# Hybrid decoder layer on one core: the step-size product with upper and lower weight parts side by side

## The chip, the cores and the metric

The kernel runs on one core of a Trainium2 chip. A core has TensorE (PE in the profile), VectorE (DVE), ScalarE (ACT), GpSimd (POOL) and SyncE (SP, which here only issues transfers). Each engine works through its own list of instructions in order; semaphores hold an instruction until what it needs is done. The metric is the time of one execution in device microseconds (us). Numbers are float32 at the inputs and outputs.

## The reference

The reference is one layer of a hybrid decoder: 16 meta tokens stand ahead of 1024 tokens of width 1024, and three groups of heads work side by side on the same normalised input.

```python
hn = rmsnorm(h, mix_norm_g[i])
proj = hn @ w_in[i].astype(dt)
sb_q, sb_k, sb_v, ssm_z, ssm_xbc, ssm_dt, c_q, c_kv, k_r = jnp.split(proj, split_at, axis=-1)
o_sb = stick_breaking_attention(...)          # 8 heads of 64
o_ssm = ssd_mixer(ssm_z, ssm_xbc, ssm_dt, ...) # state space, 16 heads of 64
...
k_rope = apply_rope(k_r, cos[None], sin[None])
o_mla = mla_attention(q_mla, k_mla, v_mla, valid)  # 8 heads, latent keys
h = h + jnp.concatenate([o_sb, o_ssm, o_mla], axis=-1) @ w_out[i].astype(dt)
fn = rmsnorm(h, ffn_norm_g[i])
h = h + (jax.nn.silu(fn @ w_gate[i]) * (fn @ w_up[i])) @ w_down[i]
return rmsnorm(h, final_norm_g)[:, BLOCK:, :]
```

Two small outputs of the large projection matter here: `ssm_dt`, 16 columns, from which `ssd_mixer` makes the step sizes (`dt = softplus(dt_raw + dt_bias)`), and `k_r`, 32 columns, the rotary part of the latent attention's keys. `apply_rope` splits the 32 into two halves x1 and x2 and returns x1 cos - x2 sin and x1 sin + x2 cos, so each output half needs both input halves.

## The kernel before

All activations are held feature by feature: 128 features on the partitions, tokens along the free axis. To keep float32 accuracy on PE, every operand is split into an upper part in a shorter float format (`hi`, the rounded value) and a lower part (`lo`, the remainder), and a product is three matmuls: upper times upper, lower weight times upper input, upper weight times lower input. The normalised input is held as eight upper tiles `HH` and eight lower tiles `HL`. `dense_fm` (L136) does a product: for each chunk of tokens, eight steps along the 1024 features with three matmuls each (L144, L145, L146) into one bank of PSUM (`d_ps`, two banks in turn), and then an evacuation that the caller gives. `load_w` (L126) brings a weight block by DMA, ACT makes the upper part (L131), POOL the lower one (L133).

The tokens (1040 with the meta tokens) go in three chunks, `CH_ALL`: 272, 384 and 384.

`step_sizes` (L419) computes the step sizes and the rotary keys together. Its weight block has 96 columns: 16 for the steps, 16 of zeros, 32 for the keys, and the same 32 again with their two halves swapped. Per chunk 24 matmuls make a result of 96 rows. In the evacuation ACT adds the bias to the 16 step rows (`dtx`, L425), copies all 96 rows (`krt`, L427) and sends rows 32 to 96 to the scratch `s_kr` in HBM (L428); PE then transposes the steps block by block into the PSUM tile `dtt` (L431). Behind the last chunk a polynomial of some 20 small instructions on DVE with two on ACT makes the softplus (L435 to L458).

Much later, before the latent attention's projections, SP loads `s_kr` (64 rows) and a table of cosines and sines (L894, L895), DVE multiplies rows 0 to 32 and the swapped rows 32 to 64 with the table and adds them (L896 to L898), and the turned keys go to `s_krot` (L899).

Around this product stands the first part of the stick-breaking attention: `sb_row` makes scores on PE (`sc_ps`, L692, L693), a sigmoid on ACT (L694) and a running product on DVE (L696); `weighted_values` multiplies the weights with the values. Between, `dense_fm` makes K and Q of the next pair of heads; `k_evac` (L600) casts and subtracts each K chunk twice, on ACT (L604, L605) and DVE (L606, L607). The order on every engine is set by a scheduler that simulates the program when it is built and takes the readiest instruction by priority; `tc.high_priority` moves an evacuation forward. So an edit in one place can change the order in others.

The later stages are: the convolutions and the other pairs (to some 440 us), the state-space stage with the latent projections as filling work (to some 640 us), the latent attention, the output product and the feed-forward part.

## Time and profile before

| what | value |
|---|---|
| median of three runs | 1745.81 us (1743.37 to 1752.36) |
| profiled execution | 1744.0 us, its span 1742.3 us, mean granted PE clock 0.989 |
| PE busy | 1688.7 us, 97% of the span |
| DVE, ACT, POOL busy | 1140.2, 846.0, 717.3 us |
| DMA | 222.35 MB, mean 128 GB/s |
| PE idle 480 to 640 us | 6.5 us |

The span is the time between the first and the last instruction that the profiler recorded. A row of a group gives the line, the engine, the operation with output and inputs, the shape and the count, the busy time, and the idle time ahead of it with what ended it. Rows in order of time begin with start and length in us; matmul lengths overlap, so the distance of two starts is what one costs. A form such as 128*96 is the part of PE's array in use, rows by columns. DVE's idle time costs nothing by itself; it matters where PE waits for DVE.

### The profile page before, as it was taken

The numbers are of one execution on the slowest core, as the hardware profiler recorded it, in microseconds if no ns is written. First come the engines' busy times: TensorE is split into PE (matmuls) and PEld (weight loads), VectorE is DVE, ScalarE is ACT, GpSimd is POOL, SyncE is SP. The second block draws the span as 40 slices with busy tenths as digits, with TensorE's granted clock in tenths as the row PEclk, the third lists the DMA queues.
The fourth block names the chain that finished last, engine by engine and source line by source line (L and its number), as shares of the span: only waits on it lengthen the run. The fifth ranks groups of instructions, "written<-read, shape, count | busy, mean of one in ns | idle before, by whom it ended". The sixth has DMA issues, their size and how long they took to land.

```text
span 1742.3 us, 26429 instructions
## 1 busy us (share of the span) xinstructions
PE 1688.7 (97%) x9673; PEld 1479.6 (85%) x9673; DVE 1140.2 (65%) x1773; ACT 846.0 (49%) x1811; POOL 717.3 (41%) x514
## 2 busy tenths in 40 slices
PE   8889999999999999999999999999999999999998
PEld 7879989999987888998888878788888888878887
DVE  7777676678455644556576556966666656688644
ACT  6555565656477727776455425432223222343333
POOL 3233335344567537553331445635555555200012
PEclk9999999999999999999999999999999999999999
DMA  4321232122534465348222452232322233999602
GB/s 164 72 67 62 69 89 80 59 69 78 154 115 121 149 219 167 107 130 282 68 78 65 103 180 73 70 99 92 114 91 97 96 104 106 328 398 358 235 1 98
DMA packets 145639, 222.35 MB, mean 128 GB/s; under 512 B 24722, under 2 KB 84148, under 8 KB 145508
## 3 DMA queue, kind: packets, MB, share of 16 engines
q1 hardware_dynamic: 126112, 205.09, 36.6%
q10 hardware_dynamic: 19396, 15.56, 2.9%
q8 instruction: 76, 1.25, 0.3%
q14 instruction: 55, 0.45, 0.1%
HBM read 157.56 MB, written 63.04 MB: 127 GB/s over the span
## 4 chain that ended last, share of the span: by engine, by line
PE 80%; DVE 6%; DMA 6%; ACT 3%; issue 2%; POOL 2%; SPq 0%; ACTq 0%; DVEq 0%; POOLq 0%
PE d_ps L144 9%; PE d_ps L146 9%; PE d_ps L145 9%; PE b_ps L1283 8%; PE b_ps L1282 8%; PE b_ps L1281 8%; PE b_ps L1566 2%; PE b_ps L1567 2%; PE b_ps L1565 2%; PE ptg L326 2%; PE ptg L328 1%; PE pv L305 1%; PE pv L304 1%; DMA raw<-s_osbl 1%; PE sc_ps L991 1%
## 5 line engine op out<-in xcount | busy, mean ns | idle before, releaser
L144 PE MATMUL d_ps<-hnh,whi 128*128 128x384 f32 (+6 forms) x744 | 247.4, 333 | 7.8 <-DVE KS L607 5.4
L146 PE MATMUL d_ps<-hnl,whi 128*128 128x384 f32 (+6 forms) x744 | 248.4, 334 | 0.0
L145 PE MATMUL d_ps<-hnh,wlo 128*128 128x384 f32 (+6 forms) x744 | 246.7, 332 | 0.1
L133 POOL TENSOR_TENSOR wlo<-wraw,whi 128x1024 fp32r<-128x1024 f32 (+1 forms) x57 | 136.8, 2401 | 218.2 <-ACT whi L131 194.1
L144 PEld LDWEIGHTS d_ps<-hnh,whi 128*128 128x128 f32 (+1 forms) x744 | 141.0, 190 | 12.7 <-issue 6.0
L146 PEld LDWEIGHTS d_ps<-hnl,whi 128*128 128x128 f32 (+1 forms) x744 | 140.8, 189 | 3.1 <-issue 0.7
L145 PEld LDWEIGHTS d_ps<-hnh,wlo 128*128 128x128 f32 (+1 forms) x744 | 140.9, 189 | 2.8 <-POOL wlo L133 0.4
L1282 PE MATMUL b_ps<-T,wl 128*128 128x512 f32 x352 | 139.6, 397 | 1.3 <-POOL wl L1113 1.3
L1283 PE MATMUL b_ps<-T,wh 128*128 128x512 f32 x352 | 139.2, 397 | 1.3 <-DVE T L1113 1.3
L1281 PE MATMUL b_ps<-T,wh 128*128 128x512 f32 x352 | 139.3, 397 | 0.0
L312 DVE TENSOR_TENSOR pl<-ptg,ph 128x512 fp32r<-128x512 f32 (+1 forms) x160 | 99.8, 628 | 55.3 <-ACT ph L311 54.1
L1112 ACT CAST op<-raw 128x1024 fp32r<-128x1024 f32 x69 | 71.2, 1050 | 111.3 <-PE d_ps L1567 55.1
L311 ACT CAST ph<-ptg 128x512 fp32r<-128x512 f32 (+1 forms) x160 | 85.6, 542 | 52.3 <-PE ptg L328 32.8
L1113 DVE TENSOR_TENSOR op<-raw,op 128x1024 fp32r<-128x1024 f32 x69 | 84.9, 1240 | 39.5 <-ACT op L1112 39.4
L696 DVE TENSOR_TENSOR_SCAN cm<-cm,sb_mask 128x144 f32<-128x144 f32 (+3 forms) x64 | 97.1, 1523 | 7.4 <-ACT cm L694 6.8
L1113 POOL TENSOR_TENSOR wlo<-raw,whi 128x1024 fp32r<-128x1024 f32 x18 | 45.4, 2521 | 110.3 <-ACT whi L1112 110.3
L1113 POOL TENSOR_TENSOR wl<-raw,wh 128x512 fp32r<-128x512 f32 x46 | 74.9, 1635 | 30.5 <-ACT wh L1112 30.3
L1112 ACT CAST wh<-raw 128x512 fp32r<-128x512 f32 x88 | 53.2, 616 | 69.5 <-PE b_ps L1283 69.4
L131 ACT CAST whi<-wraw 128x1024 fp32r<-128x1024 f32 (+1 forms) x57 | 58.9, 1033 | 55.4 <-PE d_ps L146 30.6
L1119 POOL TENSOR_TENSOR tt<-tt 128x512 f32<-128x512 f32 (+1 forms) x8 | 8.1, 1015 | 188.4 <-ACT tt L1637 188.2
L1282 PEld LDWEIGHTS b_ps<-T,wl 128*128 128x128 f32 x352 | 66.8, 190 | 17.4 <-POOL wl L1113 1.6
L1116 DVE TENSOR_TENSOR raw<-raw 128x512 f32<-128x512 f32 x58 | 53.2, 925 | 43.3 <-DMA raw<-in_w_gate_dram 38.4
(440 smaller groups left out, 5120.0 us busy)
## 6 DMA issues: line engine op xcount, KB each, us to landing
raw<-in_w_down_dram SPq DMA_DIRECT2D x99, 256.0 KB, 5.3
s_hops<-gs SPq DMA_DIRECT2D x63, 256.0 KB, 2.0
raw<-s_hops SPq DMA_DIRECT2D x63, 256.0 KB, 5.4
raw<-in_w_gate_dram SPq DMA_DIRECT2D x22, 512.0 KB, 3.6
raw<-in_w_up_dram SPq DMA_DIRECT2D x22, 512.0 KB, 4.2
wraw<-in_w_o_dram SPq DMA_DIRECT2D x16, 512.0 KB, 3.8
wraw<-in_w_xbc_dram SPq DMA_DIRECT2D x12, 512.0 KB, 4.2
s_xs<-csig SPq DMA_DIRECT2D x24, 192.0 KB, 2.6
```

Source lines behind the costliest of these rows:

```text
L133: pool.tensor_tensor(lo[:, :cols], raw[:, :cols], f32(hi[:, :cols]), op=ALU.subtract)
L144: pe.matmul(ps[:m, :n], wh, mh, start=(kt == 0), stop=False)
L145: pe.matmul(ps[:m, :n], wl, mh, start=False, stop=False)
L146: pe.matmul(ps[:m, :n], wh, ml, start=False, stop=(kt == nkt - 1))
L311: act.copy(ph[:, :n], pt[:, :n])
L312: dve.tensor_tensor(pl[:, :n], pt[:, :n], f32(ph[:, :n]), op=ALU.subtract)
L696: dve.tensor_tensor_scan(rev, rev, sb_mask[:, T - n_all :][:, ::-1], 1.0, ALU.mult, ALU.max)
L1112: act.copy(hi, value)
L1113: eng.tensor_tensor(lo, value, f32(hi), op=ALU.subtract)
L1281: pe.matmul(banks[j], hi[:, ks], UH[u][k], start=start and k == 0, stop=False, skip_group_check=skip)
L1282: pe.matmul(banks[j], lo[:, ks], UH[u][k], start=False, stop=False, skip_group_check=skip)
L1283: pe.matmul(banks[j], hi[:, ks], UL[u][k], start=False, stop=stop and k == 3, skip_group_check=skip)
```

## The change

The weight block of the step-size product has 64 columns now: 16 for the steps, 16 of zeros and 32 for the keys, without the swapped copy. Its upper and lower parts lie side by side, 64 and 64 columns, in one tile. One matmul with all 128 columns against the upper input makes the upper-weight product in rows 0 to 64 of the bank and the lower-weight product in rows 64 to 128; a second matmul with the 64 upper columns against the lower input adds to rows 0 to 64. That is two matmuls a step, not three. The evacuation copies rows 64 to 128 to SBUF on ACT, adds them to rows 0 to 64 on DVE, adds the bias to the 16 step rows on ACT and sends 32 rows to `s_kr`. The load of the keys is three transfers now, which put the two halves a second time, swapped, under the first.

```diff
-    s_kr = dram.tile([64, T], F32, name="s_kr")
+    s_kr = dram.tile([32, T], F32, name="s_kr")
...
-        def dt_evac(ps, c0, n):
-            dtx = fill_tile("cacc", "dtx")
-            act.activation(dtx[:16, :n], ps[0:16, :n], AF.Identity, bias=dtb)
-            krt = fill_tile("csig", "krt")
-            act.copy(krt[:96, :n], ps[:96, :n])
-            act.dma_start(s_kr[:, c0 : c0 + n], krt[32:96, :n])
...
-        dense_fm(dpool, load_w(a["w_dt"], KT * 96), KT, 96, hn_mov, CH_ALL, dt_evac)
+        raw = wa.tile([128, 1024], F32, tag="wraw", bufs=1, name="wraw")[:, : KT * 64].rearrange("p (k m) -> p k m", k=KT)
+        both = wa.tile([128, 1024], F32R, tag="whi", name="wdt").rearrange("p (k e m) -> p k e m", k=KT, e=2)
+        sp.dma_start(raw, a["w_dt"].rearrange("p (k m) -> p k m", k=KT))
+        act.copy(both[:, :, 0], raw)
+        pool.tensor_tensor(both[:, :, 1], raw, f32(both[:, :, 0]), op=ALU.subtract)
+        for c0, n in CH_ALL:
+            ps = bank()
+            for kt in range(KT):
+                mh, ml = hn_mov(kt, c0, n)
+                whole = both[:, kt].rearrange("p e m -> p (e m)")
+                if kt > 0:
+                    pe.matmul(ps[:64, :n], both[:, kt, 0], ml, start=False, stop=False)
+                pe.matmul(ps[:, :n], whole, mh, start=(kt == 0), stop=(kt == KT - 1))
+                if kt == 0:
+                    pe.matmul(ps[:64, :n], both[:, kt, 0], ml, start=False, stop=False)
+            with tc.high_priority(offset=1000):
+                low = fill_tile("cacc", "low")[:64]
+                act.copy(low[:, :n], ps[64:128, :n])
+                krt = fill_tile("csig", "krt")[:64]
+                dve.tensor_tensor(krt[:, :n], ps[:64, :n], low[:, :n], op=ALU.add)
+                dtx = fill_tile("cacc", "dtx")
+                act.activation(dtx[:16, :n], krt[0:16, :n], AF.Identity, bias=dtb)
+                act.dma_start(s_kr[:, c0 : c0 + n], krt[32:64, :n])
...
-        sp.dma_start(kx[0:64], s_kr)
+        for r0, r1, h0 in ((0, 32, 0), (32, 48, 16), (48, 64, 0)):
+            sp.dma_start(kx[r0:r1], s_kr[h0 : h0 + r1 - r0])
...
-    wdt96 = np.concatenate([wdt, zero, wkr, wkr[:, 16:], wkr[:, :16]], axis=1)
+    wdt64 = np.concatenate([wdt, zero, wkr], axis=1)
```

The scheduler places the instructions anew. On PE, in the first chunk of the product, this stood before (`hnh` and `hnl` are the upper and lower input, `whi` and `wlo` the parts of the weights):

```order
L144 MATMUL d_ps<-hnh_129,whi 96x272
L145 MATMUL d_ps<-hnh_129,wlo 96x272
L146 MATMUL d_ps<-hnl_137,whi 96x272
L144 MATMUL d_ps<-hnh_130,whi 96x272
L145 MATMUL d_ps<-hnh_130,wlo 96x272
L146 MATMUL d_ps<-hnl_138,whi 96x272
```

and this stands there now (`wdt` is the tile with both parts):

```order
L434 MATMUL d_ps<-hnl_138,wdt 64x272
L435 MATMUL d_ps<-hnh_130,wdt 128x272
L434 MATMUL d_ps<-hnl_139,wdt 64x272
L435 MATMUL d_ps<-hnh_131,wdt 128x272
L434 MATMUL d_ps<-hnl_140,wdt 64x272
L435 MATMUL d_ps<-hnh_132,wdt 128x272
```

Two matmuls a step took the place of three, and widths of 64 and 128 take turns. On ACT, where the first K chunk of the next pair is cast and the polynomial's exponential needs its table, the order before was (`d` is the polynomial's argument, `cm` a row of sigmoids, `ph` the upper part of the weights):

```order
L604 CAST K<-d_ps 64x272
L605 CAST KS<-d_ps 64x272
L443 ACT_TABLE_LOAD
L443 ACTIVATE d_1005<-d_1005 128x144
L360 CAST V<-vst 16x2x64 x2
L604 CAST K<-d_ps 64x272
L605 CAST KS<-d_ps 64x272
L694 ACT_TABLE_LOAD
L694 ACTIVATE cm<-sc_ps 128x256
L694 ACTIVATE cm<-sc_ps 128x400
L311 CAST ph<-ptg 128x384
```

and now (lines behind the edit are 15 higher: L619 is the K cast, L709 the sigmoid, L458 the exponential):

```order
L360 CAST V<-vst 128x8x64
L619 CAST K<-d_ps 64x272
L620 CAST KS<-d_ps 64x272
L619 CAST K<-d_ps 64x272
L620 CAST KS<-d_ps 64x272
L709 ACTIVATE cm<-sc_ps 128x256
L709 ACTIVATE cm<-sc_ps 128x400
L311 CAST ph<-ptg 128x384
L709 ACTIVATE cm<-sc_ps 128x384
L457 ACTIVATE d_986<-dx 128x144
L458 ACT_TABLE_LOAD
L458 ACTIVATE d_986<-d_986 128x144
```

Three sigmoids and a cast moved ahead of the exponential's table load, and a cast of values stands ahead of the K casts. On DVE, from the division by 2 + d on, the order before was:

```order
L447 RECIPROCAL d_1006<-d_1006 128x144
L606 TENSOR_TENSOR K<-d_ps,K 64x272
L607 TENSOR_TENSOR KS<-d_ps,K 64x272
L448 TENSOR_TENSOR d_1005<-d_1005,d_1006 128x144
L696 SCALAR_TENSOR_TENSOR cm<-cm,sb_mask 128x656
L312 TENSOR_TENSOR pl<-ptg,ph 128x384
L449 TENSOR_TENSOR d_1006<-d_1005 128x144
L450 TENSOR_SCALAR DT<-d_1006 128x144
L606 TENSOR_TENSOR K<-d_ps,K 64x384
L607 TENSOR_TENSOR KS<-d_ps,K 64x384
L452 SCALAR_TENSOR_TENSOR DT<-DT,d_1006 128x144
L696 SCALAR_TENSOR_TENSOR cm<-cm,sb_mask 128x784
```

and now:

```order
L462 RECIPROCAL d_987<-d_987 128x144
L621 TENSOR_TENSOR K<-d_ps,K 64x384
L622 TENSOR_TENSOR KS<-d_ps,K 64x384
L711 SCALAR_TENSOR_TENSOR cm<-cm,sb_mask 128x784
L463 TENSOR_TENSOR d_986<-d_986,d_987 128x144
L621 TENSOR_TENSOR K<-d_ps,K 64x384
L622 TENSOR_TENSOR KS<-d_ps,K 64x384
L464 TENSOR_TENSOR d_987<-d_986 128x144
```

The polynomial's steps moved behind the second K chunk's subtractions. The state-space stage, at 440 to 560 us, is placed anew too; its instructions are the same.

## The prediction

> **What bounds the kernel now.** I read the page first (engine totals and the chain of waits), then the busy time in stretches, then what PE waited for.

> ```profile
> PE 1688.7 (97%) x9673; PEld 1479.6 (85%) x9673; DVE 1140.2 (65%) x1773; ACT 846.0 (49%) x1811; POOL 717.3 (41%) x514
> PE 80%; DVE 6%; DMA 6%; ACT 3%; issue 2%; POOL 2%; SPq 0%; ACTq 0%; DVEq 0%; POOLq 0%
> 73.00:88.00 15.00, 15.00 (x87) 13.73 (x86) 3.18 (x4) 3.65 (x11) 5.18 (x6) 0.85 0.43 84
> 91.50:115.50 24.00, 19.74 (x95) 16.96 (x96) 21.17 (x35) 14.86 (x30) 11.11 (x10) 0.93 0.25 67
> 132.00:460.00 328.00, 325.14 (x2258) 314.81 (x2258) 234.84 (x339) 194.78 (x447) 130.67 (x100) 1.00 0.25 72
> 480.00:640.00 160.00, 153.51 (x1117) 127.66 (x1116) 92.57 (x159) 105.39 (x301) 96.02 (x68) 1.00 0.46 146
> 600.00:640.00 40.00, 36.37 (x209) 30.69 (x209) 21.31 (x32) 13.01 (x23) 13.37 (x7) 1.00 0.61 218
> ```

> In a row of stretches the columns after the length are PE, PEld, DVE, ACT and POOL, then the granted clock. PE is busy 97% of the span and is 80% of the chain, so a matmul saved is time saved unless a wait takes its place. The stage of the change, 73 to 88 us, is pure PE: 15.00 of 15.00 us, with DVE and ACT nearly idle. Right behind it the picture turns: from 91.5 to 115.5 us DVE is busy 21.17 of 24 us and PE has holes. From 132 to 460 us PE is full again (325.14 of 328), so what is won ahead of 132 us is carried to 460 us. The state-space stage (480 to 640 us) leaves PE 6.5 us idle, which bounds what a new order there could win; 3.6 of it lie in the last 40 us.

> **What the product costs.** The product's matmuls, by the trace in order of time (start, length, instruction):

> ```profile
> 72.44 0.58 PE L692 MATMUL sc_ps<-K,Q 128*128 128x256 f32 x1 [6.03 <-ACT cm L694]
> 73.49 0.43 PE L144 MATMUL d_ps<-hnh,whi 128*96 128x272 f32 x1
> 73.71 0.43 PE L145 MATMUL d_ps<-hnh,wlo 128*96 128x272 f32 x1
> ...
> 77.51 0.28 PE L144 MATMUL d_ps<-hnh,whi 128*96 128x272 f32 x1
> 77.63 0.29 PE L145 MATMUL d_ps<-hnh,wlo 128*96 128x272 f32 x1
> ...
> 78.26 0.34 PE L144 MATMUL d_ps<-hnh,whi 128*96 128x384 f32 x1
> 78.43 0.34 PE L145 MATMUL d_ps<-hnh,wlo 128*96 128x384 f32 x1
> ```

> Lengths overlap in the pipeline, so the price is the distance of starts: 0.175 us for 384 columns, 0.125 for 272, and 0.227 for 272 right after the 6.03 us of idle (the granted clock of 73 to 88 us is 0.85: the first 4.9 us after the idle run at half speed, until about 77.3). The new matmuls are 128 or 64 weight columns wide instead of 96. For that:

> ```profile
> 145.44 0.28 PE L305 MATMUL pv<-pl,V 128*64 128x256 f32 x1
> 145.56 0.28 PE L304 MATMUL pv<-ph,V 128*128 128x256 f32 x1
> 145.68 0.28 PE L305 MATMUL pv<-pl,V 128*64 128x256 f32 x1
> ```

> Matmuls 64 and 128 weight columns wide take turns here and start every 0.12 us for 256 streamed columns, next to 0.125 for 272 with 96: the price follows the streamed columns, not the width. So 24 of 72 matmuls go at full price. First chunk: 24 matmuls took 73.49 to 78.26 = 4.77 us; 16 at half speed take 3.63 and end at 77.1, still inside the slow spell, which saves 1.1. Second and third chunk: 8 fewer each, 16 x 0.175 = 2.8. **Term 1: -3.9 us.** Bounds: -3.8 (all at full speed) and -4.6 (all of the first chunk's eight at half speed); the alternation as a cost is a rival below.

> **The evacuation.** Per chunk ACT did a biased copy and a 96-row copy; now ACT copies the lower half, DVE adds it, ACT adds the bias. The nearest rows of the shapes:

> ```profile
> 83.06 0.57 ACT L425 ACTIVATE dtx<-d_ps,dtb 16x384 f32<-16x384 f32 x1 [1.56 <-PE d_ps L146]
> 83.54 0.45 ACT L427 COPY krt<-d_ps 96x384 f32<-96x384 f32 x1
> 99.47 0.47 ACT L604 CAST K<-d_ps 64x384 fp32r<-64x384 f32 x1
> 101.40 0.55 DVE L606 TENSOR_TENSOR K<-d_ps,K 64x384 fp32r<-64x384 f32 x1
> ```

> Before: 0.57 + 0.45; after: 0.47 + 0.55 until the bank is free, 0.57 more until the transposes may start. The bank comes free as early as before; the transposes' operand comes about 1.0 us later, under the next chunk's sixteen matmuls (2.8 us), and DVE, which takes the add, is busy only 3.18 of the stage's 15 us. Nothing on the path: 0, and about 1 us per chunk (3 us) if that cover were gone. The weights' cast and subtraction shrink by a third, ahead of use: 0.

> **The load of the keys.** Two more issues stand on SP's queue, ahead of the table's load:

> ```profile
> 458.86 0.47 SPq L894 DMA_DIRECT2D kx<-s_kr  x1
> 459.38 0.59 SPq L895 DMA_DIRECT2D ktab<-in_k_tab_dram  x1
> 466.91 1.23 DVE L898 TENSOR_TENSOR kx<-kx,ky 32x1040 f32<-32x1040 f32 x1
> 469.31 1.23 DVE L751 CAST sel<-seli 80x2048 bf16<-80x2048 f32 x1 [1.17 <-DMA xs<-s_xs]
> ```

> An issue takes 0.52 us, so the table and DVE's three products come 1.04 us later and end at 469.2 instead of 468.14. The next DVE instruction waits until 469.31 for another transfer anyway. 0, or up to +1.0 if that slack of 1.17 shrinks.

> **The list behind the product.** PE's two waits for DVE before 116 us, and what ACT, DVE and POOL did:

> ```profile
> 106.96 0.47 PE L144 MATMUL d_ps<-hnh,whi 128*128 128x512 f32 x1 [2.69 <-DVE KS L607]
> 115.50 0.47 PE L144 MATMUL d_ps<-hnh,whi 128*128 128x512 f32 x1 [0.74 <-DVE KS L607]
> 87.97 0.62 ACT L360 CAST V<-vst 128x512 fp32r<-128x512 f32 x1 [3.98 <-POOL vst L414]
> 93.14 1.28 ACT L443 ACT_TABLE_LOAD   x1
> 93.16 0.43 DVE L606 TENSOR_TENSOR K<-d_ps,K 64x272 fp32r<-64x272 f32 x1 [1.26 <-ACT KS L605]
> 94.79 0.92 DVE L446 TENSOR_SCALAR d<-d 128x144 f32<-128x144 f32 x1 [0.76 <-ACT d L443]
> 104.36 1.30 DVE L452 SCALAR_TENSOR_TENSOR DT<-DT,d 128x144 f32<-128x144 f32 x1
> 111.28 2.23 DVE L454 TENSOR_SCALAR DT<-DT 128x144 f32<-128x144 f32 x1
> 113.54 0.31 DVE L455 SCALAR_TENSOR_TENSOR DT<-dx,DT 128x144 f32<-128x144 f32 x1
> 114.80 0.56 DVE L607 TENSOR_TENSOR KS<-d_ps,K 64x384 fp32r<-64x384 f32 x1
> 111.02 2.40 POOL L133 TENSOR_TENSOR wlo<-wraw,whi 128x1024 fp32r<-128x1024 f32 x1 [1.32 <-ACT whi L131]
> ```

> PE's start at 115.50 is set by DVE's list, which runs from 93.16 to 115.36: K's subtractions mixed with the step sizes' polynomial. The list begins when PE's first K chunk is out, so term 1 moves it; but on ACT a cast of values stands between, which waited for POOL until 87.97 and whose feeding transfers do not move: it ends at 88.6, and two K casts of at most 0.47 us behind it end at 89.5, where term 1 alone would have them end at 89.24 (the table load begins behind them at 93.14, less 3.9): +0.3. Within the list nothing is added (its three additions fall ahead of it). DVE's idle 0.76 us waited for the exponential behind a table load; now sigmoids, a scan and a subtraction stand ahead of that step and fill it: -0.8. Two steps are stretched, 1.30 and 2.23 us where a neighbour takes 0.31, 2.9 us in all; the long one ends with POOL's subtraction (113.42). Each step now meets POOL at another moment; I take half, -1.4, between 0 and -2.9, or +2.9 if as many more are hit. **Term 2: +0.3 - 0.8 - 1.4 = -1.9 us**, from -3.4 (PE's waits of 2.69 and 0.74 gone) to +3.9 (PE's whole gain waited away).

> **State-space stage.** The scheduler also reorders 440 to 560 us: early groups stand behind two to three us more of dense matmuls, and from the twelfth group on the places agree again. Work and tail are the same: 0, between -3 and +10.6 (below).

> The sum: -3.9 - 1.9 = -5.8 us against the profiled execution's 1744.0 us (span 1742.3 and 1.7 around it): 1738.2. The median of the runs, 1745.81, lies 1.8 above it, so on the runs' scale I predict **1740 us**.

> **Rivals.**
> 1. *A wait takes the place.* DVE's list keeps its length or grows by hits from POOL, and PE, earlier at the second Q chunk, waits there instead. 21.17 busy of 24 us speak for it; against it, the list's head moves with PE's K chunk. With +2.9 in place of -1.4 the sum is -1.5: about 1744 (1743 to 1746).
> 2. *Switching width drains PE.* The widths change 14 times per chunk, 42 times in all. The transposes, of another shape, show what a change can cost:

> ```profile
> 82.11 0.33 PE L145 MATMUL d_ps<-hnh,wlo 128*96 128x384 f32 x1
> 82.37 0.30 PE L431 MATMUL dtt<-identr,dtx 16*16 16x16 f32 x3
> ```

> 0.26 us instead of 0.175, so 0.085 a change; 42 of them are 3.6 us and leave -5.8 + 3.6 = -2.2: 1744. The even 0.12 us at 145 us speaks against it. [...]
> 3. *The holes close.* Both waits go (term 2 at -3.4), the half-speed spell behind them too (granted clock 0.93 of 24 us: 1.7), and the state-space stage gives 3 of its 6.5: -12.0, 1734. For it: DVE alone causes them; against it: DVE stays nearly as full.
> 4. *Slower: the state-space groups run short of cover.* Dense matmuls used early are missing between the fifth and twelfth group, where a group's own chain (POOL, ACT, DVE) is then bare on PE. If two such groups each leave 3.6 us idle, as the stage's end does now, and a half-speed spell of 1.7 as above behind it, that is +10.6; it decides from +5.8 on. -5.8 + 10.6 = +4.8: 1751. For it: PE already idles 6.5 us there; against it: the places agree again from the twelfth group on.

> **How the numbers follow.** Forecast 0.56 (its own range 1735 to 1744), rival 1 0.20, rival 2 0.03, rival 3 0.12, rival 4 0.09. About 0.5%, 8.7 us, is what a measurement of this kernel can tell from no change. Faster by more: rival 3 and the forecast's tail, 0.17; slower by more: rival 4 with a third such group, 0.05; within: 0.78. The range from 1731 to 1749 holds the forecast, rivals 1 and 2, most of rival 3 and a part of rival 4.

> **What would show it.** Right: 48 matmuls with starts 0.175 us apart in the second and third chunk; DVE's list under 22 us long and the second Q chunk starting 5 to 6 us before 115.50; PE's idle in the state-space stage near 6.5 us. Wrong: starts 0.26 us apart at width changes; waits on DVE's K subtractions that grow by what PE saved; holes of over 2 us between the fifth and twelfth group.

## The result, and the profile after

The changed kernel takes 1755.57 us (median of 9 runs, 1753.65 to 1757.82), the kernel before beside it 1747.06 (9 runs, 1743.37 to 1752.36). The ratio is 1.0052 [1.0037, 1.0067]: slower by half a per cent, where 1740 us was forecast and 1749 was the upper end. The profiled execution took 1754.85 us with a span of 1753.1, which is 10.85 more than the profiled execution before (1744.0); the medians differ by 8.5.

The page's engine totals and its chain of waits, after:

```profile
PE 1690.6 (96%) x9649; PEld 1478.2 (84%) x9649; DVE 1141.9 (65%) x1776; ACT 845.7 (48%) x1811; POOL 721.8 (41%) x514
PE 70%; DVE 11%; DMA 6%; ACT 5%; issue 4%; POOL 3%; SPq 1%; ACTq 0%; DVEq 0%; POOLq 0%
```

There are 24 matmuls fewer, as the change says, and yet PE is busy 1.9 us longer; DVE's share of the chain goes from 6% to 11%. The busy time in stretches, after (columns as above):

```profile
73.00:88.00 15.00, 15.00 (x89) 13.68 (x87) 4.02 (x7) 5.94 (x14) 5.33 (x7) 0.83 0.42 83
91.50:115.50 24.00, 19.10 (x82) 15.97 (x82) 19.78 (x32) 13.23 (x26) 11.20 (x9) 0.86 0.28 82
132.00:460.00 328.00, 323.67 (x2235) 312.80 (x2234) 233.08 (x334) 193.16 (x445) 129.37 (x100) 0.99 0.25 72
480.00:640.00 160.00, 150.35 (x1096) 123.05 (x1094) 89.61 (x150) 105.78 (x302) 98.54 (x69) 1.00 0.45 142
1060.00:1160.00 100.00, 95.38 (x419) 76.47 (x420) 83.15 (x104) 41.61 (x69) 53.77 (x33) 0.95 0.23 72
```

The last of these stretches before:

```profile
1060.00:1160.00 100.00, 97.40 (x418) 78.58 (x417) 88.91 (x110) 42.49 (x73) 55.98 (x33) 0.95 0.21 65
```

The stage of the product is as full as before. Behind it the granted clock is 0.86 where it was 0.93; PE loses 1.5 us of busy time between 132 and 460 us, 3.2 in the state-space stage and 2.0 at 1060 to 1160.

Stretches of equal times hold different work once a kernel is shifted. So I matched the instructions of PE of two traces by what they do and their turn, and took how much later each starts than in the kernel before (both set to zero at 40 to 60 us; medians of each stretch). A falling number is a gain, a rising one a loss:

| us later than before at | 83–88 | 100–106 | 140–200 | 250–440 | 632–640 | 700–780 | 1030–1045 | 1180–1380 | 1640–1700 |
|---|---|---|---|---|---|---|---|---|---|
| after | -3.9 | -5.8 | -3.1 | 0.5 | 5.7 | 6.6 | 6.5 | 9.9 | 10.2 |

The change wins 5.8 us up to 106 us, and then loses 2.7 at 106 to 126 us, 3.6 at 215 to 241, 5.2 in the state-space stage, 0.9 behind it, 3.4 at the start of the feed-forward stage, and 0.2 between. The sum is +10.2 of the 10.85. Each loss is looked at in turn.

**The gain.** The product's matmuls in the second and third chunk, after (start, length, instruction):

```profile
78.31 0.34 PE L434 MATMUL d_ps<-hnl,wdt 128*64 128x384 f32 x1
78.48 0.34 PE L435 MATMUL d_ps<-hnh,wdt 128*128 128x384 f32 x1
78.66 0.34 PE L434 MATMUL d_ps<-hnl,wdt 128*64 128x384 f32 x1
```

They start 0.17 and 0.18 us apart with 64 and 128 weight columns in turn, as with 96 before.

**The loss at 106 to 126 us.** The second Q chunk, at 115.50 before, starts at 110.80. Directly ahead of it stands the matmul of the running sums (`acum`), first before and then after:

```profile
114.25 0.51 PE L464 MATMUL acum<-d,tri 128*128 128x144 f32 x2
...
109.54 0.85 PE L479 MATMUL acum<-d,tri 128*128 128x144 f32 x2 [3.15 <-DVE d L473]
110.80 0.76 PE L144 MATMUL d_ps<-hnh,whi 128*128 128x512 f32 x1 [0.41 <-DVE KS L622]
```

That wait of PE and three successive stretches of 3.41 us, after (the first number behind the length is PE's busy time, the granted clock is the third from the end):

```profile
PE acum L479 <- DVE d L473: 3.2, 1, 3.2
105.33:108.74 3.41, 1.06 (x5) 0.54 (x3) 3.33 (x5) 1.53 (x3) 3.03 (x2) 1.00 0.25 29
108.74:112.16 3.42, 2.21 (x5) 1.66 (x6) 2.78 (x7) 0.42 (x1) 0.00 (x0) 0.50 0.33 129
112.16:115.57 3.41, 3.41 (x9) 2.63 (x8) 0.69 (x1) 0.16 (x1) 0.00 (x0) 0.50 0.00 0
```

The running sums need the steps that DVE's list computes; PE, which has fewer matmuls ahead of them and does the first Q chunk at full speed now, is 8 us ahead there and waits 3.2 us. It is busy for only 1.06 of 3.41 us, and then two stretches run at half speed, over most of the second Q chunk. In the kernel before there is one such stretch here, of 3.41 us from 108.13, over the first Q chunk.

**The loss at 215 to 241 us.** 1.0 us of it goes in small pieces at 215 to 225, 1.0 in one wait at 234 us and 1.5 in a half-speed spell behind that wait. A weight load of 512 KB and the cast that waits for it, and what PE then waits for, first before and then after:

```profile
224.62 0.36 SPq L129 DMA_DIRECT2D wraw<-in_w_sbq_dram  x1
228.41 1.05 ACT L131 CAST whi<-wraw 128x1024 fp32r<-128x1024 f32 x1 [2.82 <-DMA wraw<-in_w_sbq_dram]
...
PE d_ps L144 <- DVE KS L607: 1.9, 1, 1.9
```

```profile
223.16 0.36 SPq L129 DMA_DIRECT2D wraw<-in_w_sbq_dram  x1
227.90 1.05 ACT L131 CAST whi<-wraw 128x1024 fp32r<-128x1024 f32 x1 [4.16 <-DMA wraw<-in_w_sbq_dram]
...
PE d_ps L144 <- DVE KS L622: 2.9, 1, 2.9
```

The load is issued 1.46 us earlier, but from issue to cast it takes 4.74 us, not 3.79, and PE's wait behind it grows from 1.9 to 2.9 us. The DMA queues in those 4.7 us, after, show one transfer more that does not belong to the kernel's data (count, MB, share of 16 engines):

```profile
q8 instruction: 1, 0.02, 2.0%
```

The profile names that queue `instruction`: 76 transfers of 16 KB (1.25 MB) in the whole program, for 2 x 9649 instructions of PE alone, so one in about 254 instructions of PE; with PE's semaphore instructions counted in, 256 start between two transfers on average, before and after. After, one runs from 1.03 us behind the load's issue for 1.51 us; before, it began 2.56 us ahead of the issue and was over. The longer wait leaves PE busy for 1.01 us of the 3.41 from 235.04, and the next stretch, from 238.45, runs at half speed; before, PE was busy for 1.56 us of the 3.41 from 234.42, and the granted clock stayed 1.00. The pieces at 215 to 225 are lost in the kernels whose weight load holds a code transfer (0.8 to 1.2 us) and in the others not (0.2 at most); why was not tried.

**The loss in the state-space stage.** Of PE's waits from 440 to 645 us, these lines grew; before, and after:

```profile
PE yd L841 <- DVE L L821: 1.2, 3, 0.7
...
PE R L794 <- ACT L L806: 1.0, 2, 0.7
```

```profile
PE yd L856 <- DVE L L836: 2.6, 2, 1.3
PE R L809 <- ACT L L821: 2.5, 6, 0.5
PE d_ps L144 <- ACT lrow L750: 1.5, 1, 1.5
...
PE yd L856 <- DVE dec L812: 1.0, 2, 0.6
...
PE yd L856 <- DVE ea L841: 0.5, 1, 0.5
```

2.2 us became 8.1; the other lines give 1.1 of it back. No wait is long, the granted clock is 1.00: many groups each wait 0.5 to 1.5 us for their own chain.

**The loss at the start of the feed-forward stage.** DVE in order of time, before and after (`hT` is the residual input, `raw` the scaled one, `sq` a sum of squares):

```profile
1059.03 2.72 DVE L1153 SCALAR_TENSOR_TENSOR hT<-hT,gffn,d_ps 128x512 f32<-128x512 f32 x4 [0.20 <-PE d_ps L173]
1061.67 1.53 DVE L1119 TENSOR_TENSOR sq<-sq 128x512 f32<-128x512 f32 x1
1063.12 1.78 DVE L1113 TENSOR_TENSOR raw<-hT,raw 128x512 fp32r<-128x512 f32 x1
```

```profile
1067.70 2.47 DVE L1135 TENSOR_TENSOR sq<-sq 128x512 f32<-128x512 f32 x1 [1.80 <-ACT sq L1411]
1070.10 2.71 DVE L1169 SCALAR_TENSOR_TENSOR hT<-hT,gffn,d_ps 128x512 f32<-128x512 f32 x4
1072.73 1.33 DVE L1129 TENSOR_TENSOR raw<-hT,raw 128x512 fp32r<-128x512 f32 x1
```

The addition of the squares stands ahead of the four scalings now; it waits 1.80 us for ACT, and four instructions that were ready wait with it. PE then waits 1.17 us for `raw` and 0.50 for a square, and the half-speed spell behind this place lasts 6.83 us, where it lasted 3.41 before: some 2 us are lost ahead of the spell and 1.5 more in it.

### The profile page after: what moved, and what is told of

It reads as the page before. It is cut to its first block, busy times and chain, and to the rows that moved or that the text cites. A ratio compares the mean times of both kernels' runs of the same rounds, so it can differ in the third digit from the quotient of the medians.

```text
span 1753.1 us, 26377 instructions
## 1 busy us (share of the span) xinstructions
PE 1690.6 (96%) x9649; PEld 1478.2 (84%) x9649; DVE 1141.9 (65%) x1776; ACT 845.7 (48%) x1811; POOL 721.8 (41%) x514
## 3 DMA queue, kind: packets, MB, share of 16 engines
q8 instruction: 76, 1.25, 0.3%
## 4 chain that ended last, share of the span: by engine, by line
PE 70%; DVE 11%; DMA 6%; ACT 5%; issue 4%; POOL 3%; SPq 1%; ACTq 0%; DVEq 0%; POOLq 0%
PE d_ps L144 8%; PE d_ps L146 8%; PE d_ps L145 8%; PE b_ps L1297 6%; PE b_ps L1298 6%; PE b_ps L1299 6%; PE b_ps L1582 2%; PE b_ps L1583 2%; PE b_ps L1581 2%; PE ptg L326 2%; PE ptg L328 1%; PE pv L305 1%; PE pv L304 1%; ACT L L821 1%; DMA raw<-s_hops 1%
## 5 line engine op out<-in xcount | busy, mean ns | idle before, releaser
L144 PE MATMUL d_ps<-hnh,whi 128*128 128x384 f32 (+4 forms) x720 | 241.2, 335 | 7.0 <-DVE KS L622 4.7
L146 PE MATMUL d_ps<-hnl,whi 128*128 128x384 f32 (+4 forms) x720 | 240.2, 334 | 0.0
L145 PE MATMUL d_ps<-hnh,wlo 128*128 128x384 f32 (+4 forms) x720 | 239.0, 332 | 0.6 <-POOL wlo L133 0.6
L133 POOL TENSOR_TENSOR wlo<-wraw,whi 128x1024 fp32r<-128x1024 f32 (+1 forms) x56 | 134.7, 2406 | 211.4 <-ACT whi L131 211.3
L144 PEld LDWEIGHTS d_ps<-hnh,whi 128*128 128x128 f32 x720 | 136.9, 190 | 11.5 <-issue 6.1
L145 PEld LDWEIGHTS d_ps<-hnh,wlo 128*128 128x128 f32 x720 | 137.1, 190 | 4.1 <-issue 1.2
L146 PEld LDWEIGHTS d_ps<-hnl,whi 128*128 128x128 f32 x720 | 137.0, 190 | 3.0 <-issue 0.7
L131 ACT CAST whi<-wraw 128x1024 fp32r<-128x1024 f32 (+1 forms) x56 | 58.1, 1038 | 57.8 <-PE d_ps L146 32.6
L1299 PEld LDWEIGHTS b_ps<-T,wh 128*128 128x128 f32 x352 | 66.4, 189 | 16.8 <-DVE T L1129 1.6
```

The costliest lines, as they stand in the source:

```text
L133: pool.tensor_tensor(lo[:, :cols], raw[:, :cols], f32(hi[:, :cols]), op=ALU.subtract)
L144: pe.matmul(ps[:m, :n], wh, mh, start=(kt == 0), stop=False)
L145: pe.matmul(ps[:m, :n], wl, mh, start=False, stop=False)
L146: pe.matmul(ps[:m, :n], wh, ml, start=False, stop=(kt == nkt - 1))
L1299: pe.matmul(banks[j], hi[:, ks], UL[u][k], start=False, stop=stop and k == 3, skip_group_check=skip)
```

## The experiments

The theory on seeing this: the change itself does what was forecast, and what it wins is lost in four places where the new arrival, or the order that the scheduler made of it, meets something. The questions were which part of the change makes which loss, and whether an order exists that keeps the gain. All kernels below ran beside the kernel before. Each ratio is the one on record, with its 95% interval; the quotient of the two medians can differ from it by 0.1% (e5: 1.0048, e10: 0.9978, e11: 0.9961). How much later PE is than in the kernel before, by the same matching:

| | ratio, 95% | 100–106 | 140–200 | 250–440 | 632–640 | 1030–1045 | 1180–1380 |
|---|---|---|---|---|---|---|---|
| after | 1.0052 [1.0037, 1.0067] | -5.8 | -3.1 | 0.5 | 5.7 | 6.5 | 9.9 |
| e1 | 1.0032 [1.0020, 1.0045] | 0.5 | 1.0 | 2.7 | 8.2 | 8.1 | 7.7 |
| e2 | 1.0052 [1.0032, 1.0073] | -6.2 | -4.0 | -0.7 | 7.3 | 12.1 | 11.7 |
| e3 | 1.0018 [1.0001, 1.0034] | -6.7 | -5.8 | -4.1 | 6.1 | 5.6 | 5.2 |
| e4 | 1.0050 [1.0028, 1.0072] | -7.1 | -3.4 | -1.8 | 4.8 | 10.0 | 9.7 |
| e5 | 1.0037 [1.0020, 1.0054] | -3.2 | -2.5 | -2.5 | 2.6 | 7.0 | 10.3 |
| e6 | 0.9988 [0.9976, 1.0001] | -6.7 | -5.8 | -1.9 | -3.1 | 0.9 | 0.5 |
| e7 | 0.9993 [0.9981, 1.0005] | -2.4 | -1.6 | -1.5 | -0.7 | -1.0 | -2.2 |
| e8 | 1.0027 [1.0013, 1.0040] | 2.8 | 4.7 | 4.6 | 3.5 | 5.3 | 4.8 |
| e9 | 1.0025 [1.0011, 1.0039] | -7.1 | -5.8 | -2.1 | 4.4 | 8.7 | 7.7 |
| e10 | 0.9968 [0.9955, 0.9981] | -7.3 | -6.3 | -6.1 | -4.8 | -0.6 | -1.0 |
| e11 | 0.9949 [0.9931, 0.9967] | -5.9 | -7.0 | -3.6 | -4.4 | 0.7 | 0.4 |
| e12 | 0.9954 [0.9940, 0.9969] | -6.2 | -7.7 | -7.7 | -7.8 | -3.5 | -2.4 |

The last columns come from one execution each, the ratios from several. Differences of 1 to 3 us in them need not be the edit's: e1, which does the work of the kernel before (but for a smaller store) in the order of the kernel before up to 460 us, stands at 1.0 and 2.7, because half-speed spells fall at other places (one of 3.41 us from 239.2, behind a wait of 1.97 us, where the kernel before has none).

### The load of the keys alone (e1)

The kernel before, with the 32-row store and the three loads:

```diff
-    s_kr = dram.tile([64, T], F32, name="s_kr")
+    s_kr = dram.tile([32, T], F32, name="s_kr")
-            act.dma_start(s_kr[:, c0 : c0 + n], krt[32:96, :n])
+            act.dma_start(s_kr[:, c0 : c0 + n], krt[32:64, :n])
-        sp.dma_start(kx[0:64], s_kr)
+        for r0, r1, h0 in ((0, 32, 0), (32, 48, 16), (48, 64, 0)):
+            sp.dma_start(kx[r0:r1], s_kr[h0 : h0 + r1 - r0])
```

> The kernel before with the change's key load alone: the product keeps its 96 columns and three matmuls a step, 32 key rows are stored, and three loads make the swapped copy. In the changed kernel PE is 2.5 us ahead of before until 220 us, 0.5 us behind from 245 us (counted from the first instruction of each), and then loses 5.2 us between 460 and 640 us, 0.9 us at 656 us and 3.5 us between 1060 and 1160 us. The instruction order of this kernel is that of the kernel before up to the state-space stage, and that of the changed kernel in it. Theory A (the order that the two extra key loads bring into the state-space stage costs the time): PE keeps the pace of before up to 460 us and is 4 to 6 us behind it at 640 us; 1751 to 1757 us against 1747 before. Theory B (the product costs it, by moving all that follows): within 2 us of before all along, 1745 to 1749 us.

Measured 1749.4 against 1744.4. Up to the state-space stage the order on every engine is that of the kernel before, and in it that of the changed kernel. PE does not quite keep the pace up to 460 us, it comes in 2.7 us late; it goes out 8.2 late, a loss of 5.5. The waits that grow from 440 to 645 us are the same as in the changed kernel:

```profile
PE yd L841 <- DVE L L821: 2.2, 2, 1.3
PE d_ps L144 <- ACT lrow L735: 2.0, 1, 2.0
PE R L794 <- ACT L L806: 2.0, 5, 0.5
```

So the two added loads bring the state-space loss, without the product being touched. What of them does it, their time on the queues or the order that the scheduler makes of them, e6 tells.

### The product alone (e2)

The product as changed, 48 rows stored (keys and their first half again), and one load that reads rows 0 to 32 and 16 to 48:

```diff
+        two = s_kr[0:32]
+        two = bass.AP(two.tensor, two.offset, [[16 * T, 2], [T, 32], [1, T]])
+        sp.dma_start(kx[0:64], two)
-    wdt64 = np.concatenate([wdt, zero, wkr], axis=1)
+    wdt64 = np.concatenate([wdt, wkr, wkr[:, :16]], axis=1)
```

> The change's product alone: 64 columns in one pass, but with the columns dt, key, first half of the key (48 key rows stored), so that one load, which reads rows 0-31 and 16-47, makes both copies. Its order is that of the changed kernel in the product, and that of the kernel before from the first running sums on. Theory A (the order in the state-space stage costs the time): 2 to 3 us ahead of before until 220 us, level with it within 1 us from 245 us to the end; 1745 to 1749 us. Theory B (the product costs it): the losses of the changed kernel at 460-640, 656 and 1060-1160 us are all there, 1753 to 1757 us. The blind prediction's own sum for this part alone would be 5.8 us less than before, 1741 us.

Measured 1753.31. The gain is there as in the changed kernel, and a half-speed spell too (3.41 us from 110.0, where the changed kernel has 6.83 from 108.7). In the state-space stage the run tells nothing about the question, because that one load was slow: the time is that of theory B, but not for its reason. Its issue, the first product on the keys, and PE's wait for the mask that stands behind it on DVE:

```profile
457.62 0.65 SPq L911 DMA_DIRECT2D kx<-s_kr  x1
470.24 1.23 DVE L913 TENSOR_TENSOR ky<-kx,ktab 32x1040 f32<-32x1040 f32 x1 [12.40 <-DMA ktab<-in_k_tab_dram]
475.18 0.38 PE L809 MATMUL R<-A,sel 80*128 80x16 bf16 x8 [5.74 <-DVE sel L766]
```

DVE stood still for 12.40 us there (5.30 before), PE for 5.74. The released operand is named as the table, which stands behind the slow load on the same queue.

### Dense matmuls in place of the idle time (e3)

e2 with 24 matmuls of 256 columns, whose output nobody reads, ahead of the running sums' matmul. From here on the order is given as a list of ranks and pinned by dependencies between successive instructions of an engine, without a semaphore, so that only the edit differs:

```diff
+        for _ in range(24):
+            pe.matmul(pt[:, :256], identr, hn_mov(0, 272, 256)[0], start=True, stop=True)
         pe.matmul(pt[:, :NC], tri, d1, start=True, stop=True)
...
+                tc.add_manual_dep(
+                    i, last[i.engine],
+                    mybir.DependencyInfo(mybir.DependencyClass.NoSync, mybir.DependencyReason.DATA),
+                    reason="order",
+                )
```

> The kernel of the product alone, in the same order on every engine, with 24 matmuls of 256 columns (0.12 us each, 2.9 us together, into the bank of the running sums, which the next matmul overwrites) ahead of the matmul of the running sums, where PE idled 3.15 us in the changed kernel. They add no wait. Theory C (the idle time itself brings the half-speed spell of 6.83 us that starts at 108.7 us): the spell is gone or half as long, and PE is 1.7 to 3.4 us further at 123 us than in the product alone. Theory D (the spell comes from the work, not from the idle time): the spell is as long as in the product alone, 0 us. Under both, what is gained before 220 us may be lost at 234 us, where PE waited 1.9 us before and 2.9 us in the changed kernel for a chain that starts with the landing of a weight load: the whole time is 0 to 2 us less than the product alone.

Measured 1747.41: adding 24 matmuls made e2 faster by 6 us, where 0 to 2 were expected. The half-speed spell ahead of 126 us is gone, as theory C has it (-5.8 at 140 to 200 us instead of -4.0, 1.8 us), and PE reaches 250 us at -4.1 instead of -0.7. So the idle time itself, not the lateness of DVE, made PE slow there. These two places do not explain the 6 us: at 632 to 640 us the two traces are 1.2 us apart, and most of the difference arises between 780 and 1045 us, where e2 waits longer for a load (it comes up again at e12).

### Later loads of the last value rows (e4)

e2 with four small loads (`vlast`), which stand on SP's queue behind the weight load of 223 us, issued after the next two value loads. Those loads were the rival for the longer weight load.

> The kernel of the product alone, in the same order on every engine but SP: the four loads of the last value rows (64x8 elements of 4 bytes each), which SP issues behind the weight load at 223 us, are issued behind the two loads of values that follow. Theory E (these small packets hold up the weight load, whose landing ends the chain of copy, subtraction and K copies on which PE waits at 234 us: 3.3 us from issue to copy in the kernel before, 4.7 in the changed one): the load lands 0.5 to 1.5 us earlier, the wait at 234 us falls from 2.9 us to below 2, no half-speed spell follows, and the time is 1.5 to 3.5 us less than the product alone. Theory F (the load's own 512 KB set its time): the landing moves by less than 0.3 us and the time by less than 0.5 us.

Measured 1.0050 of the time before, where e2 had 1.0052. The weight load still took 4.56 us from issue to cast (4.87 in e2), PE's wait 2.55 us. The small loads were not what held it.

### The count of PE's instructions, in the change's own order (e5)

The changed kernel with 24 matmuls of 16 columns ahead of the product, which put PE's instruction count back to that before, and with it the places where code is fetched:

```diff
+            if c0 == 0:
+                for _ in range(24):
+                    pe.matmul(ps[:, :16], identr, hn_mov(0, 0, 16)[0], start=True, stop=True)
```

> The changed kernel in its own order on every engine, with 24 matmuls of 16 columns put into PE's idle time at 67-72 us, so that PE again issues as many instructions as before. (Their results go into a bank that the product's first matmul overwrites.) Seen so far: a transfer of 16 KB of PE's instructions comes every 256 of them; in the kernel before it lies at 222.1-223.5 us, ahead of the weight load issued at 224.6, which lands after 3.8 us; in the changed kernel, with 24 matmuls and 24 weight loads fewer ahead of it, at 224.2-225.7 us, inside that load (issued at 223.2, 4.7 us); with 24 matmuls added at 106 us (the run without idle time) it was ahead again (215.7-217.0, load issued at 218.3, 3.7 us), and nothing was lost after 640 us. Theory G (where the code transfers fall, against the loads that PE waits for, costs time): the load takes 3.7 to 4.0 us, the wait at 234 us is about 1.9 us, and the 4.5 us that the changed kernel loses after 640 us are gone: 1.0015 to 1.0035 of the time before. Theory H (only the order in the state-space stage and the half-speed spells at 109 and 238 us cost time): as the changed kernel, 1.004 to 1.0065.

Measured 1754.08 against 1745.7. The code transfer begins 2.25 us ahead of the weight load, the load takes 3.80 us and PE's wait is 1.91, as before; from 140 to 440 us nothing is lost (-2.5 and -2.5). But the small matmuls cost some 2.6 us, and what theory G expected behind 640 us did not come: 4.4 us were lost at 640 to 1045 us and 3.3 at 1060 to 1160, which the count therefore does not explain.

### The order of before on the changed kernel (e6, e7, e8)

e6 is the changed kernel with the order of the kernel before on every engine from the first running sums on, and the three key loads in the place of the one. e7 adds 24 matmuls of 16 columns ahead of the product, e8 adds 48.

> The changed kernel, its product and its three key loads, with the order of the kernel before imposed on all engines from the first running sums on (the three key loads stand where the one stood). Theory A (the order that the three loads bring costs the 5 us of the state-space stage, not the loads): PE loses less than 1 us between 460 and 640 us, and the time is 4 to 6 us less than the changed kernel: 1.001 to 1.003 of the time before. If the loads themselves hold up the stage: 1.004 to 1.0065, as the changed kernel.

Measured 1743.79 against 1745.7: by the two ratios 11 us less than the changed kernel, with all of its work and its loads. The state-space stage in e6 (busy time of 480 to 640 us):

```profile
480.00:640.00 160.00, 154.05 (x1129) 128.83 (x1128) 93.17 (x161) 104.93 (x296) 94.77 (x68) 1.00 0.44 143
```

PE is busy for 154.05 us, 153.51 before and 150.35 after; e6 loses nothing there (-1.9 to -3.1) and nothing at 1060 to 1160. With the same three loads on the queue, both losses came from the order alone. It keeps the loss at 215 to 241 us, from -5.8 to -1.9, and between 640 and 1045 us it loses 4.0, where the changed kernel loses 0.8 (see e12).

> The kernel of the run with the order of before, with the 24 matmuls of 16 columns in PE's idle time at 67-72 us as well. Theories A and G together: the first 220 us bring 3 to 4 us, of which 0 to 2 are lost at 234 us, and nothing is lost later: 0.997 to 1.000 of the time before. If only A holds: 1.001 to 1.003. If only G holds: 1.0015 to 1.0035.

Measured 1743.98. Between e6 and e7 stand only the 24 small matmuls. The weight load goes from 5.20 us to 4.00, PE's wait from 2.72 to 1.99, and the loss at 215 to 241 us is gone (-1.6 to -1.5): that the number of PE's instructions far ahead lengthens this load is shown here, and that it does so by the code transfer agrees with all 14 traces (the table at the end). The half-speed spell is a second condition: e1 and e3 have it behind waits of 1.97 and 1.94 us, without a code transfer in the load. The gain was eaten by the small matmuls themselves:

```profile
70.75 5.26 PE L756 MATMUL d_ps<-hnh,identr 128*128 128x16 f32 x24 [4.43 <-DVE KS L949]
```

They waited 4.43 us for a bank, until 70.75, and ran at the half speed that follows this wait, 0.213 us from start to start.

> The kernel of the run with the order of before, with 48 matmuls of 16 columns in PE's idle time at 67-72 us (some 4.8 us long, so that up to 1 us may stand outside it): the code transfers fall as far ahead of their places in the kernel before as they fell behind them in the changed one. Theory G: the time differs from that with 24 by 1 to 5 us, and where it differs a code transfer lies inside a load that PE waits for in the one and outside it in the other. Theory H: the same as with 24 within 1 us.

Measured 1751.26. The 48 matmuls cost 9.5 us ahead of 100 us, where 1 at most was expected. The code transfer moved to 4.96 us ahead of the load, the load took 3.70 us, PE's wait was 1.87, as in e7; so the 7.3 us between the two runs are mostly the small matmuls, and the run does not decide between the theories.

### One addition on DVE (e9)

The changed kernel in its own order, with only the addition of squares back behind the four scalings, and the rows of PE that moved with it.

> The changed kernel in its own order, but at the start of the feed-forward part the addition of squares on DVE stands behind the four scalings of hT as in the kernel before (the changed order puts it ahead of them, where DVE then idles 1.8 us for ACT's squares), with the two PE rows that moved with it. Theory I (this one place costs the 3.5 us that the changed kernel loses between 1060 and 1160 us): those 3.5 us are gone, 2.5 to 4 us less than the changed kernel, 1.0025 to 1.004 of the time before. Theory J (the loads of that stretch set its time): as the changed kernel, 1.0045 to 1.006.

Measured 1749.65 against 1744.87. DVE at that place, with the scalings first again:

```profile
1069.44 2.73 DVE L1500 SCALAR_TENSOR_TENSOR hT<-hT,gffn,d_ps 128x512 f32<-128x512 f32 x4 [0.20 <-PE d_ps L504]
1072.08 1.35 DVE L1466 TENSOR_TENSOR sq<-sq 128x512 f32<-128x512 f32 x1
```

Nothing is lost at 1060 to 1160 us any more (8.7 becomes 7.7, where the changed kernel goes from 6.5 to 9.9), and PE's waits of 1.17 and 0.50 us are gone. So one instruction's place made that loss. The half-speed spells also fall otherwise in e9 (3.41 us in this stretch, 10.24 in the changed kernel), so how much of the 3.4 us is the waits and how much the clock is known only roughly.

### Order, idle time and count together (e10)

e6 with the 24 matmuls of 256 columns of e3, which fill the idle time ahead of the running sums and put the count back at once.

> The kernel of the run with the order of before (0.9988), with 24 matmuls of 256 columns in the 3.1 us of idle time ahead of the running sums, as in the run without idle time: they fill the idle time and restore PE's instruction count without time of their own. Theory C (a half-speed spell follows when PE idles too much in one of the 3.41 us windows in which the spells start): no spell follows the fill, 1.7 us. Theory G (code transfers): the weight load issued at about 218 us takes 3.7 to 4.0 us instead of 4.6, the wait that follows is 1.9 us instead of 2.7: 1 to 3 us. Both: 0.9955 to 0.9975 of the time before. C alone: 0.997 to 0.9985; neither: 0.998 to 1.000.

Measured 1741.06 against 1744.87, 0.9968 [0.9955, 0.9981]: faster than the kernel before. The stretches around 105 us in e10:

```profile
101.30:104.70 3.40, 3.40 (x17) 2.76 (x16) 3.25 (x7) 2.08 (x4) 2.99 (x2) 1.00 0.16 41
104.70:108.10 3.40, 2.91 (x26) 2.71 (x24) 3.23 (x6) 1.34 (x3) 2.22 (x2) 1.00 0.33 93
108.10:111.50 3.40, 2.66 (x11) 2.09 (x12) 2.67 (x5) 0.58 (x1) 0.00 (x0) 1.00 0.15 61
```

The granted clock stays 1.00, the weight load takes 3.67 us and PE's wait at 230 us is 1.94; what stands at -6.3 at 140 us is still -6.1 at 440. Behind 640 us this trace, too, loses some 4 us (-4.8 to -0.6).

### The last chunk's keys ahead of the polynomial (e11, e12)

e6 with three moves: DVE subtracts the keys of the third chunk ahead of six polynomial steps, ACT copies these keys ahead of the values, and PE's running sums stand in the second half of the Q chunk. e12 adds 24 matmuls of 16 columns in the wait ahead of the second Q chunk.

> The kernel of the run with the order of before, with three moves ahead of the second query chunk: DVE makes the key subtractions of the third chunk (after six of the polynomial's steps) before the polynomial's last steps, ACT makes the second half's key copies ahead of a values copy, and PE takes the running sums' matmul from ahead of the chunk into its second half. No matmul is added, so the code transfers stay where they were in that kernel. If DVE's list is what the second query chunk waits for: it starts 1.5 to 2 us earlier, PE's wait there is below 1.8 us in all, and no half-speed spell follows: 3 to 3.7 us gained at 121 us, of which 0 to 3 are lost at 232 us, where the weight load that holds a code transfer ends the wait (2.7 us or more): 0.997 to 0.9988. If the polynomial's delay turns into a wait of its own (the evacuation of the query chunks behind it, 2.1 us at 121 us now): 0.9985 to 1.000.

Measured 1738.10 (7 runs), 0.9949 [0.9931, 0.9967]: the fastest of all, and better than expected, but not by the way expected:

```profile
108.00 0.54 PE L475 MATMUL d_ps<-hnh,whi 128*128 128x512 f32 x1 [2.32 <-DVE KS L953]
```

The second Q chunk starts at 108.00, some 1.2 us ahead of e6's; a wait of 2.32 us and a half-speed stretch remain, and the weight load takes 4.68 us. The execution that the profiler recorded was the slowest of the seven (1744.58), so its trace does not hold the gain over e6, and where the gain comes from stays open.

> The kernel of the last run (key subtractions first, 0.9949 of the time before), with 24 matmuls of 16 columns (0.085 us each at full speed, 2.0 us) in the 2.3 us that PE still waits ahead of the second query chunk, so that PE's instruction count is that of the kernel before. In the twelve kernels profiled so far the weight load issued at 218-229 us took 3.7 to 4.0 us from its issue to its copy where no code transfer of PE lay inside it, with a PE wait of 1.9 to 2.0 us after it, and 4.6 to 5.2 us where one did, with a wait of 2.6 to 2.95 us. Theory G: the load takes 3.7 to 4.0 us, the wait is 1.9 to 2.0 us, and the time is 1 to 3 us less than without them: 0.993 to 0.9945 of the time before. If code transfers do not set it: 0.9945 to 0.9955. If the 24 matmuls do not fit the wait: 0.9955 to 0.997.

Measured 1739.41 against 1746.25, 0.9954 [0.9940, 0.9969]. The load takes 3.95 us and PE's wait is 1.96, as expected of the count, and -7.7 is carried from 140 to 640 us. But the total is not below that of e11, as theory G expected it to be (by medians both are 0.9961 of the time before). In its trace some 4 us are lost between 640 and 1045 us, most of them at 780 to 830: PE there waits 2.4 us for DVE's step on `hT`, which waits for a load, against 1.14 in the kernel before. In e2, e4, e6 and e9 to e11 this wait is 2.5 to 2.8 us, in e3 and e5 1.6 and 1.8, and in the changed kernel, e1, e7 and e8 1.2 to 1.5. That load was not tried by itself, and why it is late stays open.

## Why the prediction was wrong

By its own steps:

- **Term 1, -3.9 us: right.** PE is 3.9 us ahead at 83 to 88 us; with the same product it is 4.1 to 5.5 in e2 to e4, e6 and e9 to e12. The alternation of 64 and 128 columns costs nothing (starts 0.17 and 0.18 us apart, 0.175 before), so rival 2 falls.
- **The evacuation at 0: right.** PE stays at -3.9 up to 88 us, and at -4.7 by 92 to 100.
- **Term 2, -1.9 us: right in sign, too large.** Its place is the second Q chunk, which starts 4.7 us earlier than before on the traces' own clocks and 5.3 with both set to zero at 40 to 60 us, against a sum of 5.8. DVE's list runs from 89.23 to 110.65, 21.4 us instead of 22.2: 0.8 less, where 0.8 + 1.4 was counted; steps of 1.35 and 1.25 us still stand in it. That PE is 5.8 us ahead at 100 to 106 us, ahead of that place, is partly luck: with the same product the other traces show 5.9 to 7.3 there. Rival 1 came in part: PE does wait for DVE's list at the second Q chunk, not at the K subtractions (1.7 us in all) but at the running sums (3.2 us). Its price did not come, since the list did not keep its length.
- **"What is won ahead of 132 us is carried to 460 us": the step that failed first.** It was drawn from PE being busy for 325 of 328 us. But the gain was already down to -3.1 at 140 us and was +0.5 at 250. The sum let the list set the start of the second Q chunk, but put at nothing what PE's idle time ahead of it does to the clock: 3.2 us of waiting made the half-speed spell twice as long (6.83 us, 3.41 before) and moved it over that chunk. The spell's removal was counted only in rival 3, its growth nowhere. Then one weight load in the "full" stretch met a code transfer (4.74 us instead of 3.79), and behind PE's longer wait for it (2.91 us instead of 1.94) came 3.41 us at half speed. Being full did not mean that nothing could be late: 6.3 us were lost at these two places, more than the 5.8 won (e10, which mends both, carries 6.1 of its 6.3).
- **The load of the keys at 0 to +1.0: failed in kind.** The added issues were priced on SP's queue at 1.04 us, and even that was too much: from the first issue to the first key product it takes 5.52 us before, 5.65 after and 5.87 in e6, and e6 with the three loads loses nothing in that stage. What the loads cost is the order that the scheduler makes when they are there: 5.2 us in the state-space stage.
- **The state-space stage at 0: failed.** Rival 4 named this stage and its sign at 0.09 and +10.6; it was half of that, in many waits of 0.5 to 1.5 us and not in two of 3.6, and without the half-speed spell that it carried. "Work and tail are the same" was true, and the same work in the other order waited 4.8 us longer.
- **The feed-forward stage: not in the sum at all.** The order listing was read up to 560 us; one addition that moved past four scalings at 1067 us cost 3.4.
- **Rival 3 (the holes close): did not come.** The holes of this list moved to another wait.

So the arithmetic of the product was right, that of DVE's list right to about 1 us, and the error of 16 us in the traces (+10.2 in place of -5.8) is made of what the order and the arrival did behind it: 6.3 + 5.2 + 3.4 and 1.0 of small ones, which were not looked into. With the order of before the same change is 1743.79 against 1745.7; with the idle time filled as well it is 0.9968 of the time before, a gain of 5.6 us by that ratio and of 3.8 by the medians.

## What to carry to other kernels

When a scheduler places the program anew, a local saving is the smaller part of the answer: compare the order of every engine to the end of the program, and for each instruction that moved ahead of others ask what it waits for and who is queued behind it. To learn what an edit itself is worth, pin the old order on the new work; here that was worth 11 us. A saving ahead of a stall can lengthen the stall: here it grew to 3.2 us, and the clock ran at half speed for 6.83 us behind it. Matmuls that nobody needs, put into that hole, then brought 1.8 us at that place (e3 against e2), and e10, where they restore the count as well, is by the ratios 3.5 us faster than e6. Put behind a wait of 4.43 us they brought nothing in the total: 24 of them (e7) cost 4.3 us ahead of 106 us and end at 0.9993 of the time before, where e6 ends at 0.9988; 48 (e8) cost 9.5 us and end at 1.0027.

## What the runs showed of the hardware

**Code transfers beside loads.** The weight load at 217 to 229 us, from issue to cast, and the code transfer nearest to it:

| | load, us | code transfer begins, from the issue (length) | PE's wait behind it |
|---|---|---|---|
| before | 3.79 | -2.56 (1.39) | 1.94 |
| after | 4.74 | +1.03 (1.51) | 2.91 |
| e1 | 3.96 | -2.80 (0.89) | 1.97 |
| e2 | 4.87 | +1.22 (1.48) | 2.81 |
| e3 | 3.72 | -2.57 (1.26) | 1.94 |
| e4 | 4.56 | +1.18 (1.28) | 2.55 |
| e5 | 3.80 | -2.25 (1.11) | 1.91 |
| e6 | 5.20 | +1.07 (1.44) | 2.72 |
| e7 | 4.00 | -2.54 (0.96) | 1.99 |
| e8 | 3.70 | -4.96 (1.37) | 1.87 |
| e9 | 4.95 | +2.85 (0.89) | 2.73 |
| e10 | 3.67 | -2.16 (0.96) | 1.94 |
| e11 | 4.68 | +1.53 (0.93) | 2.95 |
| e12 | 3.95 | -2.55 (1.12) | 1.96 |

Without one inside, the load takes 3.67 to 4.00 us; with one, 4.56 to 5.20. So 24 matmuls fewer at 75 us made a load at 223 us slower. When the load was issued, from 216.85 us in e12 to 229.46 in e8, does not sort the two groups.

**A load whose rows overlap.** e2's single load of 64 rows, 16 of them read twice, kept DVE waiting 7 us longer than the plain load of 64 rows (12.40 us, 5.30 before). Whether the overlap or the other store did it was not tried.
